# A column sum over 32,768 rows: float32 loads folded in place instead of loads that cast to float16

## The chip, the cores and the metric

The kernel runs on one core of a Trainium2 chip. A core has five engines with their own instruction queues: TensorE (PE in the profile; PEld is its weight load), VectorE (DVE), ScalarE (ACT), GpSimd (POOL) and SyncE (SP). Any of SP, ACT and POOL can issue a DMA; 16 DMA engines carry them out. The metric is the device time of one execution in microseconds (us), the median of several runs.

## The reference

```python
batch, seq, dim = 32, 1024, 2048
grad_output = randn(batch, seq, dim)            # float32
out = np.sum(grad_output, axis=(0, 1))          # float32, 2048 numbers
```

The input is seen as a matrix of 32,768 rows and 2048 columns, 268.4 MB; the output is the sum of each column, 8 KB.

## The kernel before

**The layout.** SBUF has 128 partitions, so 128 rows are one row block; there are 256 blocks of 1.05 MB of float32. A load of `m` blocks puts `m` consecutive rows into each partition, one contiguous run of `m` times 8 KB in memory. To add over the 128 partitions, TensorE multiplies the data with a column of ones (L161): the result is one row of 512 column sums in PSUM. Four PSUM banks (`accs`, L110) hold the four quarters of the 2048 columns, and every matmul accumulates into its bank, from the first with `start` to the last with `stop`.

**The plan (L60 to L85).** A list of loads is made first and then carried out in order (L132 to L168):

- two single blocks in float32, issued by SP (`PRE_TILES`, L62), with tiles of their own;
- thirty loads of eight blocks, and a remainder of two blocks, issued by POOL into float16 tiles `t` (L67): the DMA casts on the way, so that half of what is read is written;
- a taper of four and two blocks (`BULK_TAPER`, L72);
- five single blocks (`TAIL_TILES`, L76);
- the last block in four column pieces, the last quarter first (L80).

Three buffers (`T_BUFS`) take the loads of several blocks. The framework derives all waits between engines from what each instruction reads and writes.

**The work on a tile.** For a tile of several blocks VectorE adds its second half to its first (L152, float16 in and out, into one of three tiles `c`), which halves what TensorE must read; then one matmul (L161) for every 512 columns of `c`: sixteen for eight blocks. A single block goes to TensorE without an add. A buffer is free for the next load as soon as the add at L152 has read it, and POOL's issue (L146) waits for that.

**The end.** Four copies bring the banks from PSUM to the SBUF row `res`, on ScalarE (L175) and VectorE (L177) in turn, the last quarter first; SP stores the 8 KB (L178).

Of the kernel before, what the change touches and what calls it, by code (L numbers as in the profile page):

```python
# [1 line left out]

# [4 lines left out]

P = 128
MM_N = 512  # L10

PRE_TILES = 2
PRE_M = 1
PRE_ENGS = ("sync", "sync")
BULK_M = 8
BULK_TAPER = (4, 2)
USE_DVE = True
TAIL_TILES = 5
COL_SPLIT_LAST = True
T_BUFS = 3  # L20
C_BUFS = 3
TAIL_BUFS = 8
BULK_ENGS = ("gpsimd",)
OUT_COPY_ENGS = ("scalar", "vector")


@with_exitstack
def kernel(
    ctx: ExitStack,
    tc: tile.TileContext,  # L30
    grad_output: bass.AP,
    out: bass.AP,
):
    nc = tc.nc
    fp32 = mybir.dt.float32
    fp16 = mybir.dt.float16

    D = out.shape[-1]
    flat = grad_output.rearrange("b s d -> (b s) d")
    R = flat.shape[0]  # L40
    assert R % P == 0 and D % MM_N == 0
    nbanks = D // MM_N
    n_row_blocks = R // P

    pre_tiles = min(PRE_TILES, n_row_blocks // PRE_M // 4)
    col_split = COL_SPLIT_LAST and nbanks > 1
    taper = [m for m in BULK_TAPER if m < BULK_M]
    n_small = TAIL_TILES + (1 if col_split else 0)
    while pre_tiles * PRE_M + sum(taper) + n_small > n_row_blocks:
        if TAIL_TILES and n_small > 1:  # L50
            n_small -= 1
        elif taper:
            taper = taper[1:]
        else:
            col_split = False
            n_small = min(n_small, 1)
            break
    n_tail = n_small - (1 if col_split else 0)

    plan: list = []  # L60
    row = 0
    for i in range(pre_tiles):  # L62
        plan.append((row, PRE_M, fp32, PRE_ENGS[i % len(PRE_ENGS)], 0, D))
        row += P * PRE_M
    tail_start = R - P * (n_small + sum(taper))
    bi = 0
    while row < tail_start:  # L67
        take = min(P * BULK_M, tail_start - row)
        plan.append((row, take // P, fp16, BULK_ENGS[bi % len(BULK_ENGS)], 0, D))
        bi += 1  # L70
        row += take
    for m in taper:  # L72
        plan.append((row, m, fp16, BULK_ENGS[bi % len(BULK_ENGS)], 0, D))
        bi += 1
        row += P * m
    for _ in range(n_tail):  # L76
        plan.append((row, 1, fp16, BULK_ENGS[bi % len(BULK_ENGS)], 0, D))
        bi += 1
        row += P
    if col_split:  # L80
        for b in range(nbanks - 1, -1, -1):
            plan.append((row, 1, fp16, BULK_ENGS[bi % len(BULK_ENGS)], b * MM_N, MM_N))
            bi += 1
        row += P
    assert row == R  # L85

    io_pool = ctx.enter_context(tc.tile_pool(name="io", bufs=T_BUFS))
    pre_pool = None
    if pre_tiles:
        pre_pool = ctx.enter_context(tc.tile_pool(name="pre", bufs=pre_tiles))  # L90
    c_pool = None
    if USE_DVE:
        c_pool = ctx.enter_context(tc.tile_pool(name="csum", bufs=C_BUFS))
    n_small_tiles = n_tail + (nbanks if col_split else 0)
    tail_pool = None
    if n_small_tiles:
        tail_pool = ctx.enter_context(
            tc.tile_pool(name="tail", bufs=min(n_small_tiles, TAIL_BUFS))
        )
    const_pool = ctx.enter_context(tc.tile_pool(name="const", bufs=1))  # L100
    psum_pool = ctx.enter_context(tc.tile_pool(name="psum", bufs=1, space=bass.MemoryType.PSUM))

    ones16 = const_pool.tile([P, 1], fp16)
    nc.vector.memset(ones16[:], 1.0)  # L104
    ones32 = None
    if pre_tiles:
        ones32 = const_pool.tile([P, 1], fp32)
        nc.vector.memset(ones32[:], 1.0)  # L108

    accs = [  # L110
        psum_pool.tile([1, MM_N], fp32, tag=f"psum{b}", name=f"psum{b}")
        for b in range(nbanks)
    ]
    res = const_pool.tile([1, D], fp32)

    def uses_dve(entry) -> bool:
        _, m, dt_, _, _, col_n = entry
        return USE_DVE and dt_ is fp16 and m > 1 and col_n == D

    def n_chunks(entry) -> int:  # L120
        _, m, dt_, _, _, col_n = entry
        n = (m * col_n) // MM_N
        return n // 2 if uses_dve(entry) else n

    total_mm = [0] * nbanks
    for e in plan:
        for j in range(n_chunks(e)):
            total_mm[((e[4] + j * MM_N) % D) // MM_N] += 1
    started = [False] * nbanks
    n_mm = [0] * nbanks  # L130

    for i, entry in enumerate(plan):  # L132
        row0, m, dt_, eng_name, col_lo, col_n = entry
        rows = flat[row0 : row0 + m * P]
        if col_n == D:
            src = rows.rearrange("(p m) d -> p (m d)", p=P)
        else:
            src = rows[:, col_lo : col_lo + col_n]

        if dt_ is fp16:  # L140
            big = m > 1 and col_n == D
            pool, tag = (io_pool, "T") if big else (tail_pool, "Ttail")
            T = pool.tile([P, m * col_n], fp16, tag=tag, name=f"t{i}")
        else:
            T = pre_pool.tile([P, m * col_n], fp32, tag="Tpre", name=f"t{i}")
        getattr(nc, eng_name).dma_start(out=T[:], in_=src)  # L146

        red = T
        if uses_dve(entry):
            half = (m * col_n) // 2  # L150
            C = c_pool.tile([P, half], fp16, tag="C", name=f"c{i}")
            nc.vector.tensor_tensor(  # L152
                out=C[:], in0=T[:, :half], in1=T[:, half:], op=mybir.AluOpType.add
            )
            red = C

        w = ones16 if dt_ is fp16 else ones32
        for j in range(n_chunks(entry)):
            b = ((col_lo + j * MM_N) % D) // MM_N
            n_mm[b] += 1  # L160
            nc.tensor.matmul(  # L161
                accs[b][:, :],
                lhsT=w[:],
                rhs=red[:, j * MM_N : (j + 1) * MM_N],
                start=(not started[b]),
                stop=(n_mm[b] == total_mm[b]),
            )
            started[b] = True  # L168

    bank_order = list(range(nbanks - 1, -1, -1)) if col_split else list(range(nbanks))  # L170
    for k, b in enumerate(bank_order):
        eng = OUT_COPY_ENGS[k % len(OUT_COPY_ENGS)]
        dst = res[:, b * MM_N : (b + 1) * MM_N]
        if eng == "scalar":
            nc.scalar.copy(out=dst, in_=accs[b][:, :])  # L175
        else:
            nc.vector.tensor_copy(out=dst, in_=accs[b][:, :])  # L177
    nc.sync.dma_start(out=out[None, :], in_=res[:])  # L178


# [1 line left out]
_INS = ['grad_output']  # L182
_OUTS = [((2048,), 'float32')]


# [23 lines left out]
```

## Time and profile before

The times of three runs were 629.38, 629.17 and 629.12 us; the median is 629.17 us. The profiled execution has a span of 627.2 us from its first to its last instruction. The median lies 2.0 us above that; the list of times does not say which of its values belongs to the profiled execution.

| | before |
|---|---|
| median of the runs | 629.17 us |
| span of the profiled execution | 627.2 us |
| written into SBUF by DMA | 135.36 MB, mean 216 GB/s |
| mean granted clock of TensorE | 0.650 of full speed |
| 8-block loads, issue to landing | 53.1 us (median of 30) |
| add at L152, 128x8192 | 4425 ns, 30 times |
| add at L152, 128x4096 | 2293 ns, once |
| matmul instructions on float32, 128x512 | 16, mean 859 ns |
| matmul instructions on float16 sums, 128x512 | 496, mean 533 ns |

How to read the profile: a *busy* share is the time in which an engine executed, over the span. In the *chain that ended last*, the profile goes back from the last instruction to whatever released it, again and again; what stands there set the time. "DVE c L152" is VectorE's instruction of line 152 that writes the tile `c`; "another core or an unknown queue" is a wait whose releaser the profile can't name. In a timeline line the numbers are the start in us from the span's beginning, the busy time, the engine, the line, the operation, and in brackets how long the engine sat idle before and what ended that. In a *stage table* each line is a stretch of time with the busy time and the number of instructions of each engine, the granted clock of TensorE, the busy share of the DMA engines and the GB/s that they wrote. A lower clock makes a matmul longer: the clock switches between half and full speed.

### The profile page before, as it was taken

The numbers are of one execution on the slowest core, as the hardware profiler recorded it, in microseconds if no ns is written. First come the engines' busy times: TensorE is split into PE (matmuls) and PEld (weight loads), VectorE is DVE, ScalarE is ACT, GpSimd is POOL, SyncE is SP. The second block draws the span as 40 slices with busy tenths as digits, with TensorE's granted clock in tenths as the row PEclk, the third lists the DMA queues.
The fourth block names the chain that finished last, engine by engine and source line by source line (L and its number), as shares of the span: only waits on it lengthen the run. The fifth ranks groups of instructions, "written<-read, shape, count | busy, mean of one in ns | idle before, by whom it ended". The sixth has DMA issues, their size and how long they took to land.

```text
span 627.2 us, 1267 instructions
## 1 busy us (share of the span) xinstructions
PE 195.1 (31%) x536; PEld 58.1 (9%) x536; DVE 138.9 (22%) x37; ACT 2.4 (0%) x3; POOL 22.6 (4%) x46
## 2 busy tenths in 40 slices
PE   3323320333203333123341134321333312343165
PEld 0001100011000111001110011100111000111011
DVE  0202222022220122211222202222022221122320
ACT  0000000000000000000000000000000000000000
POOL 1000000000000000000000000000000000000110
PEclk9677556775567665667655776656676567665677
DMA  9999999999999999999999999999999999999997
GB/s 242 226 234 201 234 201 234 202 232 203 232 203 232 203 232 203 232 204 230 205 230 205 230 205 230 205 230 206 228 207 228 207 224 211 224 211 221 206 206 139
DMA packets 6344, 135.36 MB, mean 216 GB/s; under 512 B 705, under 2 KB 1217, under 8 KB 1857
## 3 DMA queue, kind: packets, MB, share of 16 engines
q0 software_dynamic: 6048, 133.17, 98.9%
q1 hardware_dynamic: 290, 2.11, 0.9%
q8 instruction: 4, 0.07, 0.0%
q14 instruction: 2, 0.02, 0.0%
HBM read 268.44 MB, written 0.01 MB: 428 GB/s over the span
## 4 chain that ended last, share of the span: by engine, by line
another core or an unknown queue 66%; DVE 21%; DMA 11%; PE 1%; POOL 1%; issue 0%; DVEq 0%; POOLq 0%
DVE c L152 20%; DMA t<-in_grad_output_dram 11%; PE psum L161 1%; POOL t L146 1%; DVEq L152 0%; DVE res L177 0%; POOLq L193 0%
## 5 line engine op out<-in xcount | busy, mean ns | idle before, releaser
L161 PE MATMUL psum<-c,ones 128*1 128x512 f16 x496 | 175.9, 533 | 405.5 <-DVE c L152 405.5
L152 DVE TENSOR_TENSOR c<-t 128x8192 f16<-128x8192 f16 (+2 forms) x33 | 137.5, 4167 | 471.1 <-DMA t<-in_grad_output_dram 471.1
L161 PEld LDWEIGHTS <-ones 128*1 128x1 f16 x520 | 56.5, 109 | 537.5 <-issue 516.4
L146 POOL DMA_DIRECT2D t<-in_grad_output_dram x42 | 22.4, 538 | 590.4 <-DVE c L152 575.3
L161 PE MATMUL psum<-t,ones 128*1 128x512 f16 (+1 forms) x40 | 19.4, 639 | 23.5 <-DMA t<-in_grad_output_dram 23.5
L177 DVE COPY res<-psum 1x512 f32<-1x512 f32 x2 | 1.4, 679 | 13.9 <-PE psum L161 13.9
L161 PEld LDWEIGHTS psum<-t,ones 128*1 128x1 f32 x16 | 1.6, 106 | 27.5 <-DMA t<-in_grad_output_dram 14.1
L175 ACT COPY res<-psum 1x512 f32<-1x512 f32 x2 | 1.1, 575 | 621.1 <-PE psum L161 621.1
L175 ACT ACT_TABLE_LOAD x1 | 1.3, 1283 | 0.7 <-PEq L193 0.7
L104 DVE MEMSET ones<- 128x1 f16 x1 | 0.1, 59 | 0.8 <-PEq L193 0.8
L193 POOL MEMSET const-float32-0.0<- 128x1 f32 x1 | 0.1, 100 | 0.2 <-issue 0.2
L193 POOL MEMSET const-bfloat16-1.0<- 128x1 bf16 x1 | 0.1, 103 | 0.0
L193 POOL MEMSET const-float32-1.0<- 128x1 f32 x1 | 0.1, 100 | 0.0
L193 POOL MEMSET const-uint8-127<- 128x1 uint8 x1 | 0.1, 100 | 0.0
L108 DVE MEMSET ones<- 128x1 f32 x1 | 0.1, 59 | 0.0
## 6 DMA issues: line engine op xcount, KB each, us to landing
t<-in_grad_output_dram POOLq DMA_DIRECT2D x30, 4096.0 KB, 53.1
t<-in_grad_output_dram POOLq DMA_DIRECT2D x5, 512.0 KB, 20.4
t<-in_grad_output_dram SPq DMA_DIRECT2D x2, 1024.0 KB, 14.3
t<-in_grad_output_dram POOLq DMA_DIRECT2D x2, 1024.0 KB, 26.6
t<-in_grad_output_dram POOLq DMA_DIRECT2D x1, 2048.0 KB, 29.0
t<-in_grad_output_dram POOLq DMA_DIRECT2D x4, 128.0 KB, 16.1
out_dram<-res SPq DMA_DIRECT2D x1, 8.0 KB
```

The source lines that it names most:

```text
L104: nc.vector.memset(ones16[:], 1.0)
L108: nc.vector.memset(ones32[:], 1.0)
L146: getattr(nc, eng_name).dma_start(out=T[:], in_=src)
L152: nc.vector.tensor_tensor(out=C[:], in0=T[:, :half], in1=T[:, half:], op=mybir.AluOpType.add)
L161: nc.tensor.matmul(accs[b][:, :], lhsT=w[:], rhs=red[:, j * MM_N : (j + 1) * MM_N], start=(not started[b]), stop=(n_mm[b] == total_mm[b]),)
L175: nc.scalar.copy(out=dst, in_=accs[b][:, :])
L177: nc.vector.tensor_copy(out=dst, in_=accs[b][:, :])
L193: nc = _bacc.Bacc("TRN2", target_bir_lowering=False, num_devices=1)
```

## The change

The kernel is written anew around a ring, with its own semaphores in place of the derived waits.

- **Loads.** All 256 blocks are loaded as float32, without a cast, and all loads are issued by SP. The ring has three slots of eight blocks, 64 KB of each partition. The units are 29 of eight blocks, then 6, 4, 4, 2, 2, 2, 2 (`UNITS`); unit `i` goes into slot `i % 3`, and from the fourth on SP waits until the unit three before it is used up (`s_free`). The last two blocks come in three pieces: the left three quarters of the columns of both, then the last quarter of each. These use the free part of slot 2 and have no wait of their own.
- **Folds.** VectorE adds in place, float32: blocks 4 to 7 onto 0 to 3 (128x8192), then blocks 2 and 3 onto 0 and 1 (128x4096), with a wait for the first add between them. A 6-block unit adds blocks 4 and 5 onto 0 and 1 and then folds as a unit of four; a 4-block unit has only the second add; a 2-block unit has none. Two blocks are left of every unit.
- **Matmuls.** Eight float32 matmuls for a unit, two for each quarter of the columns. The quarters use four column groups of the TensorE array (`tile_position`) and write to partitions 0, 32, 64 and 96 of PSUM: quarters 0 to 2 into `acc`, quarter 3 into `accr`. Both are cleared by VectorE at the start and every matmul adds. The second four end with the increment that frees the slot; then come six float16 matmuls on zeros into a bank that nothing reads (`FILL`).
- **Loops.** VectorE's first 27 units are a loop of nine turns over the three slots; the rest is written out. TensorE's 36 units are a loop of twelve turns, six fill matmuls in every unit.
- **The end.** The left columns of the last two blocks are summed first; VectorE copies `acc` and SP stores those three quarters while the last quarter is still coming in. After the last quarter's matmuls ScalarE copies `accr` and issues the store of 2 KB itself.

All of it stands in a critical section, in which the framework adds no waits of its own; POOL leads it. The core of the new code:

```diff
+M = 8
+SLOTS = 3
+LOOPS = 9
+UNITS = (M,) * 29 + (6, 4, 4, 2, 2, 2, 2)
+FILL = 6
...
+    def take(engine, sem, n):
+        engine.wait_ge(sem, n)
+        engine.sem_inc(sem, -n)
...
+    def fold(at, n, by):
+        part = ring[:, at : at + n * D]
+        return v.tensor_tensor(
+            out=part, in0=part, in1=ring[:, at + by * D : at + (by + n) * D], op=add
+        )
...
+    def unit(s, m):
...
+        at = s * W
+        take(v, landed[s], 16)
+        if m == 2:
+            v.sem_inc(red[s], 1)
+            return
+        if m > 4:
+            fold(at, *((4, 4) if m == 8 else (2, 4))).then_inc(s_vec, 1)
+            take(v, s_vec, 1)
+        fold(at, 2, 2).then_inc(red[s], 1)
...
+    def sums(at, c0=0, w=D):
+        for g in range(4):
+            lo, hi = max(c0, g * Q), min(c0 + w, (g + 1) * Q)
+            if lo < hi:
+                mm = t.matmul(
+                    (acc if g < 3 else accr)[32 * g : 32 * g + 1, lo - g * Q : hi - g * Q],
+                    lhsT=ones[:],
+                    rhs=ring[:, at + lo - c0 : at + hi - c0],
+                    start=False,
+                    stop=False,
+                    tile_position=(0, 32 * g),
+                    skip_group_check=True,
+                )
+        return mm
...
+    with tc.tile_critical(sync_engine=lead):
...
+        for i, m in enumerate(UNITS):
+            at = i % SLOTS * W
+            src = flat[row * P : (row + m) * P].rearrange("(p m) d -> p (m d)", p=P)
+            if i >= SLOTS:
+                q.wait_ge(s_free, i - SLOTS + 1)
+            q.dma_start(out=ring[:, at : at + m * D], in_=src).then_inc(landed[i % SLOTS], 16)
+            row += m
+        src = flat[row * P :].rearrange("(p m) d -> p m d", p=P)
+        at = (SLOTS - 1) * W + 2 * D
+        left = ring[:, at : at + 6 * Q].rearrange("p (m c) -> p m c", m=2)
+        q.dma_start(out=left, in_=src[:, :, : 3 * Q]).then_inc(last[0], 16)
+        for m in range(2):
+            q.dma_start(
+                out=ring[:, at + (6 + m) * Q : at + (7 + m) * Q], in_=src[:, m, 3 * Q :]
+            ).then_inc(last[1 + m], 16)
...
+        with v.Fori(0, LOOPS) as _:
+            for s in range(SLOTS):
+                unit(s, M)
+        for i in range(LOOPS * SLOTS, len(UNITS)):
+            unit(i % SLOTS, UNITS[i])
...
+        t.wait_ge(s_one, 4)
+        with t.Fori(0, len(UNITS) // SLOTS) as _:
+            for s in range(SLOTS):
+                take(t, red[s], 1)
+                sums(s * W)
+                sums(s * W + D).then_inc(s_free, 1)
+                for _ in range(FILL):
+                    t.matmul(
+                        junk[0:1, :],
+                        lhsT=fill[:, :1],
+                        rhs=fill[:],
+                        start=True,
+                        stop=True,
+                        tile_position=(0, 0),
+                    )
+        t.wait_ge(last[0], 16)
+        sums(at, 0, 3 * Q)
+        sums(at + 3 * Q, 0, 3 * Q).then_inc(s_end[0], 1)
+        for m in range(2):
+            t.wait_ge(last[1 + m], 16)
+            mm = sums(at + (6 + m) * Q, 3 * Q, Q)
+        mm.then_inc(s_end[1], 1)
...
+        v.wait_ge(s_end[0], 1)
+        v.tensor_copy(out=res[0:96, :], in_=acc[0:96, :]).then_inc(s_res[0], 1)
+        a.wait_ge(s_end[1], 1)
+        a.copy(out=res[96:97, :], in_=accr[96:97, :]).then_inc(s_res[1], 1)
+        q.wait_ge(s_res[0], 1)
+        q.dma_start(
+            out=out[: 3 * Q].rearrange("(g c) -> g c", g=3), in_=res[0:65:32, :]
+        ).then_inc(s_out[0], 16)
+        a.wait_ge(s_res[1], 1)
+        a.dma_start(out=out[None, 3 * Q :], in_=res[96:97, :]).then_inc(s_out[1], 16)
```

## The prediction

> **What bounds the kernel now.** I read the busy shares first, then the chain that ended last, then the same chain in order of time, then the end of the timeline. The page's shares and queues:
>
> ```profile
> PE 195.1 (31%) x536; PEld 58.1 (9%) x536; DVE 138.9 (22%) x37; ACT 2.4 (0%) x3; POOL 22.6 (4%) x46
> DMA  9999999999999999999999999999999999999997
> ...
> q0 software_dynamic: 6048, 133.17, 98.9%
> q1 hardware_dynamic: 290, 2.11, 0.9%
> ...
> HBM read 268.44 MB, written 0.01 MB: 428 GB/s over the span
> ```
>
> No compute engine is busy a third of the span; the 16 DMA engines are never idle. 133 MB is written but 268 MB is read, because the bulk loads turn float32 into float16 on the way. The chain in order of time shows the beat (start, length, what):
>
> ```profile
> 46.74 4.43 DVE c L152
> 51.16 14.87 another core or an unknown queue
> 66.06 4.43 DVE c L152
> ...
> 104.81 4.42 DVE c L152
> 109.23 15.75 another core or an unknown queue
> 125.10 4.42 DVE c L152
> 129.53 14.72 another core or an unknown queue
> 144.37 4.42 DVE c L152
> ...
> 588.89 4.43 DVE c L152
> ```
>
> The "unknown queue" is the load stream: L152 starts once per 8-row tile when it lands. From 46.74 to 588.89 are 28 beats. One is long (104.81 to 125.10, 20.29 us); the other 27 average (542.15 - 20.29) / 27 = 19.33 us, or 2.416 us for one row block (128 rows, 1.05 MB read, 434 GB/s). L152 is busy 4.43 us of a beat, so its cost does not set the time. The end, from the timeline (start, busy, engine):
>
> ```profile
> 613.11 1.02 PE L161 MATMUL psum<-t,ones 128*1 128x512 f16 x4 [0.68 <-DMA t<-in_grad_output_dram]
> 615.58 1.02 PE L161 MATMUL psum<-t,ones 128*1 128x512 f16 x4 [1.45 <-DMA t<-in_grad_output_dram]
> 618.02 1.53 PE L161 MATMUL psum<-t,ones 128*1 128x512 f16 x4 [1.42 <-DMA t<-in_grad_output_dram]
> 620.52 3.57 PE L161 MATMUL psum<-t,ones 128*1 128x512 f16 x8 [0.96 <-DMA t<-in_grad_output_dram]
> 624.13 0.68 DVE L177 COPY res<-psum 1x512 f32<-1x512 f32 x1 [0.17 <-PE psum L161]
> 624.90 0.32 SPq L178 DMA_DIRECT2D out_dram<-res  x1
> ```
>
> Single blocks become usable every 2.47 us, so the last block, which follows 620.52 in four pieces, is complete near 623.0. Its matmuls end at 624.09, the last copy at 624.81, the store is issued at 624.90, and the span ends 2.3 us later at 627.2. The median run is 629.17, so 2.0 us lie around the span (629.12 to 629.38 in the list: 1.9 to 2.2); the list does not say which of them the profile belongs to. I carry 2.0 over.
>
> **The change part by part.**
>
> **The load stream.** The same 268.44 MB are read, now written as float32: 8.39 MB into SBUF for a tile instead of 4.19. No row shows 8-row loads of this kind. The nearest are the two one-block float32 loads on SP: the first was issued at 0.74 and its matmul started at 5.74; and while they run, the stage table has
>
> ```profile
> 2.00:6.00 4.00, 0.26 (x1) 0.12 (x2) 0.00 (x0) 0.02 (x1) 0.96 (x2) 1.00 1.38 438
> ```
>
> 438 GB/s landed in SBUF (last column), against the 217 of the bulk, so a doubled write is not slower by itself. Shorter slices of that stage gave 426, 426 and 415. From one side, then, the price is 268.44 MB / 426 GB/s = 630.1 us, 11.6 more than 256 x 2.416 = 618.5; from the other, the shortest beat in the fence (125.10 to 144.37, 19.27 us) gives 616.6. I take 618.5, because the read of 434 GB/s is what the bulk is paced by and it is unchanged.
>
> **The queue.** 42 issues leave POOL (22.4 us busy, off the chain). SP gets 36 loads and three pieces, and the last quarter's store goes to ScalarE's queue, behind its own copy; in front of each from the fourth on stands the wait for a free slot. Behind that wait are only later loads and the first output store, so a late slot delays the stream and nothing else. A slot comes free after two folds and eight matmuls. The trace has no float32 add. The float16 one of 128x8192 took 4425 ns and of 128x4096 2293 ns; at the same time per element both folds would be 6.7 us; at the rate of the float32 copy at L177 (679 ns for 512, 1.33 ns each) 16.3 us; at the same bytes per ns, 2 x (4.43 + 2.29) = 13.4 us. I take 13.4, the row nearest in kind; even 16.3 is under the 19.33 beat.
>
> The Trainium skill ("VectorE: DVE Perf Modes", Mode 2x_2P) says that a float32 tensor_tensor cannot leave the one-element-per-cycle mode; by its 0.96 GHz an estimate of both folds is 12.8 us, which would change nothing in the sum.
>
> **The matmuls.** A float32 one of 512 columns is two matmul instructions in the trace (16 for the two early tiles' eight). Their weight loads start 0.86 us apart up to 27.57 and 0.43 after 28.16, the two clocks. Eight per tile are then 16 x 0.86 = 13.8 us, or 6.9, if the four column groups take turns, and 4 x 0.43 = 1.7 us if four run at once at full clock (3.4 at half). No column group appears in this trace, so both stand. The six fill matmuls are 0.23 us each (16 in 3.61 us) or 0.43: 1.4 to 2.6 us. In the steady state it does not matter: 13.4 + 13.8 = 27.2 us from landing to free, plus about 2.6 from issue to data (5.74 - 0.74 less one block of 2.45), against 38.7 us that the two other slots keep the queue filled. That is the cover, 8.9 us deep.
>
> **The loops.** VectorE's nine and TensorE's twelve turns have branches that the trace does not price. The long beat is the one disturbance it shows, 0.96 us over the others. At that price TensorE's twelve would be 11.5 us if each stopped the stream, and zero if it falls in idle time; in the steady state TensorE works at most 16.4 of 19.33 us, so I take zero.
>
> A rule against the loops: the Trainium skill ("Runtime: NRT & Kernel Launch", Instruction fetch mechanics) says that a taken branch leaving the current two-page window stalls for a fetch; no run here shows one yet. By it the sum would grow only where a turn's code is longer than that window.
>
> **The short units at the end.** The last seven units are 6, 4, 4, 2, 2, 2, 2 blocks, then two blocks in three pieces. Count from when unit 28 is usable. Unit 31 is usable at 14 x 2.416 = 33.8, folded 4.4 later at 38.2. Unit 34 reuses its slot and must be issued 2.6 + 4.8 before 48.3, at 40.9: with 1.7 us of matmuls the slot is free at 39.9, with 3.4 at 41.6, 0.7 late. Unit 35 must be issued at 45.7: free at 43.0 (39.9 + 1.4 of fill + 1.7), or at 47.6 at half clock, 1.9 late. Bounds 0 to 1.9, taken 0.3, because the fills keep TensorE at 3.1 of each 4.8 us. In the stage table TensorE was busy 5.01 of 7 us from 604 to 611 and had a clock of 0.96 in the next 7 us; there it was busy 3.47 of 7, and the clock was 0.53 after 618. 64% lies between 72% and 50%, so either clock can be had.
>
> **The two ends.** The loads stand in a critical section led by POOL; SP's waits around barriers are 0.5 to 0.7 us in the list of waits, so its entry costs 0 to 0.7, taken 0.3. Last quarter: one float32 matmul, 0.86 us (1.7 at half clock) and 0.1 to hand over; ScalarE's copy 0.57 (L175); 0.1 to issue; 2.3 to the end as now. The table load (1283 ns, now at 0.74) stays early if it is ahead of ScalarE's wait; behind it, it adds 1.3. I take zero.
>
> **Sum.** 0.74 + 0.3 + 2.6 + 618.5 = 622.1; + 0.3 slots = 622.4; + 0.96 + 0.57 + 0.1 + 2.3 = 626.3. Against 627.2 that is 0.9 less: 0.6 of the last data (622.4 for 623.0) and 0.3 of the end. With 2.0 around it: 628.3 us, 0.1% under the median, inside the 0.2% (1.26 us) that I count as no change. If every bound falls well (entry and slots 0) it is 627.7; if all go badly (entry 0.7, slots 1.9, half clock, table load behind the wait) 632.5. Half of the difference between the beats of 19.33 and 19.27 lets it reach 626.8.
>
> **Rivals.**
> *TensorE becomes the bound at the end.* Place: units 31 to 35. It decides once matmuls and fills of a two-block unit exceed 4.83 us. If each matmul's second instruction must wait for its first in the same group and only neighbours overlap, eight take 9 x 0.43 = 3.9, with fills 5.2. From 38.2: five units 26.0, the left columns 3.0, two quarters 1.7, end at 68.9 against 58.9: 10.0 more, 638.3. With no overlap: 8.3 a unit, 38.2 + 41.5 + 5.2 + 1.7 = 86.6, about 656. For it: in-order issue and no row with overlap. Against it: four separate column positions. Chance 0.20 (mostly the first).
> *The stream runs at the short slices' rate.* Smaller pieces or pauses between loads on SP: up to 11.6 more, 639.9; with a third of that 632.2. For it: 426 and 415. Against it: those slices hold the first latencies. Chance 0.10.
> *Both ends and the stream gain.* The beat of 19.27 throughout gives 1.9 less, 626.4. For it: PE's unrolled stream, whose fetches I suspect in the long beat, is gone, and so are the short column pieces. Against it: 27 beats average 19.33. Chance 0.10.
>
> **How the numbers follow.** The forecast has 0.60; its own range of 626.8 to 632.5 puts 0.26 below 627.9, 0.31 within 0.2%, 0.03 above 630.4. The fast rival adds 0.10 to faster; the slow two add 0.29 to slower and 0.01 to the same. So 0.36 faster, 0.32 the same, 0.32 slower. Range 625.8 to 638.5: down past the fast rival, up to the partial overlap; no overlap and a stream at 426 are left out.
>
> **What would show it.** Beats between first folds of 19.3 us, folds near 8.9 and 4.5 us, SP never later than the queue's end, DMA at 9 in every slice; in the last 60 us, matmuls of one unit over before the next lands. It is wrong if beats are 19.5 or more, if TensorE works on after the last piece has landed for over 2 us, or if DMA shows gaps before the last units.

## The result, and the profile after

The changed kernel takes 631.11 us (median of six runs, 631.03 to 632.55) against 629.16 us for the kernel before in the same comparison (six runs, 628.64 to 629.38): a ratio of 1.0037, 95% interval 1.0025 to 1.0048. It is slower by 0.37% by that ratio (1.95 us, 0.31%, by the medians), where 628.3 us had been forecast. The profiled execution has a span of 629.3 us and took 631.03, so 1.7 us lie around it; the span itself is 2.1 us longer than the 627.2 of before.

The shares and queues on the page of the changed kernel:

```profile
PE 184.1 (29%) x808; PEld 38.9 (6%) x808; DVE 400.1 (64%) x67; ACT 1.9 (0%) x2; POOL 0.2 (0%) x4
...
DMA  9999999999999999999999999999999999999996
...
q1 hardware_dynamic: 5750, 268.44, 98.9%
...
HBM read 268.44 MB, written 0.01 MB: 427 GB/s over the span
```

VectorE went from 22% to 64% busy and POOL to nothing, and neither shows in the time: the DMA engines are at 9 in every slice but the last, as before. The beat, in the timeline of VectorE (a row is one unit's two folds, of 8.69 and 4.42 us; "DVEq L58" is the wait for a landed load in `take`):

```profile
22.96 13.26 DVE L62 TENSOR_TENSOR ring<-ring 128x8192 f32<-128x8192 f32 x2 [20.45 <-DVEq L58]
...
100.38 13.26 DVE L62 TENSOR_TENSOR ring<-ring 128x8192 f32<-128x8192 f32 x2 [6.09 <-DVEq L58]
119.73 13.27 DVE L62 TENSOR_TENSOR ring<-ring 128x8192 f32<-128x8192 f32 x2 [6.09 <-DVEq L58]
...
564.89 13.26 DVE L62 TENSOR_TENSOR ring<-ring 128x8192 f32<-128x8192 f32 x2 [6.10 <-DVEq L58]
```

From 22.96 to 564.89 are 28 beats, (564.89 - 22.96) / 28 = 19.355 us each. None is long: where before had its 20.29 us beat, this one has 119.73 - 100.38 = 19.35. VectorE waits 6.1 us in every beat, so the folds are not on the path. At 564.89 the first 29 units (232 blocks) are usable. Before, L152's thirtieth tile, with the two early blocks the 242nd block, was usable at 588.89, so 232 blocks at 588.89 - 10 x 2.416 = 564.7. So up to here the two kernels are level to 0.2 us, and the loss lies in the last 65 us. Its first half is in the timeline around unit 31:

```profile
595.41 1.46 PE L131 MATMUL junk<-fill 128*1 128x512 f16 x6
...
595.66 14.60 SPq L101 DMA_DIRECT2D ring<-in_grad_output_dram  x3
598.86 4.42 DVE L62 TENSOR_TENSOR ring<-ring 128x4096 f32<-128x4096 f32 x1 [5.31 <-DVEq L58]
...
603.42 1.03 PE L82 MATMUL acc<-ring,ones 128*1 128x512 f32 x3 [6.55 <-PEq L58]
...
604.23 1.07 PE L82 MATMUL acc<-ring,ones 128*1 128x512 f32 x3
...
605.08 1.07 PE L82 MATMUL acc<-ring,ones 128*1 128x512 f32 x3
...
605.94 0.90 PE L82 MATMUL acc<-ring,ones 128*1 128x512 f32 x3
...
607.97 0.60 PE L82 MATMUL acc<-ring,ones 128*1 128x512 f32 x3
...
608.39 0.60 PE L82 MATMUL acc<-ring,ones 128*1 128x512 f32 x3
```

TensorE had nothing to do for 6.55 us before unit 31. Its matmul instructions then start 0.81 to 0.86 us apart, at half clock; those of unit 32, from 607.5 on, 0.42. Three quarters start as one, and the fourth within 0.03 us of them: the four column groups do run at once. Unit 31's last matmul ends at 605.94 + 0.90 = 606.84, SP issues the load of unit 34 into that slot at 606.92 (the second of the three in the row at 595.66), and its first packet starts at 607.88. The stage table says what the DMA engines did meanwhile (last two columns: their busy share and GB/s):

```profile
606.50:607.00 0.50, 0.50 (x6) 0.17 (x2) 0.00 (x0) 0.00 (x0) 0.00 (x0) 0.96 0.77 328
607.00:607.50 0.50, 0.50 (x4) 0.17 (x2) 0.00 (x0) 0.00 (x0) 0.00 (x0) 1.00 0.70 295
607.50:608.00 0.50, 0.50 (x10) 0.22 (x12) 0.00 (x0) 0.00 (x0) 0.00 (x0) 1.00 1.03 229
```

A packet's time and bytes are booked where it starts, so short slices are rough; still, from the 422 GB/s of the stretch from 595 to 607 they fall to 328, 295 and 229. By the packets' own times unit 33 is in at 608.06 and unit 34 at 614.16, 6.10 us later, where two blocks cost 2 x 2.419 = 4.84: 1.26 us lost. The last packet ends at 624.23, against 622.76 before. The second half of the loss is the end, from the timeline (SPq and ACTq: issues of a DMA):

```profile
623.32 1.03 PE L82 MATMUL acc<-ring,ones 128*1 128x512 f32 x6 [0.39 <-DMA ring<-in_grad_output_dram]
...
625.27 0.69 DVE L149 COPY res<-acc 96x512 f32<-96x512 f32 x1 [21.99 <-PE acc L82]
625.89 0.58 ACT L151 COPY res<-accr 1x512 f32<-1x512 f32 x1 [623.73 <-PE accr L82]
625.99 0.84 SPq L153 DMA_DIRECT2D out_dram<-res  x1
626.50 0.50 ACTq L157 DMA_DIRECT2D out_dram<-res  x1
```

The left columns start at 623.32 and their matmuls, with the last quarter's in turn behind them, keep TensorE until 625.87, 1.64 us after the last packet. So VectorE's copy of the left columns (625.27) and SP's store of them (625.99) come after all data is in, and not while the last quarter is still on its way. By the trace's semaphore records SP's store, issued first, is also the one that lands last: at 627.90, ScalarE's at 627.67. From the last packet to the end of the span are 5.07 us; before they were 627.16 - 622.76 = 4.40.

So the 2.1 us between the two profiled executions are 0.2 up to unit 28, 1.27 from there to the last packet (1.26 of it at unit 34) and 0.67 at the end: 2.14.

### The profile page after: what moved, and what is told of

It reads as the page before. It is cut to its first block, busy times and chain, and to the rows that moved or that the text cites. A ratio compares the mean times of both kernels' runs of the same rounds, so it can differ in the third digit from the quotient of the medians.

```text
span 629.3 us, 1940 instructions
## 1 busy us (share of the span) xinstructions
PE 184.1 (29%) x808; PEld 38.9 (6%) x808; DVE 400.1 (64%) x67; ACT 1.9 (0%) x2; POOL 0.2 (0%) x4
## 5 line engine op out<-in xcount | busy, mean ns | idle before, releaser
L62 DVE TENSOR_TENSOR ring<-ring 128x4096 f32<-128x4096 f32 (+1 forms) x62 | 398.1, 6421 | 202.7 <-DVEq L58 198.3
L82 PE MATMUL acc<-ring,ones 128*1 128x512 f32 x444 | 122.8, 970 | 441.8 <-PEq L58 441.4
L82 PE MATMUL accr<-ring,ones 128*1 128x512 f32 x148 | 121.4, 969 | 0.0
L131 PE MATMUL junk<-fill 128*1 128x512 f16 x216 | 69.4, 471 | 0.0
L82 PEld LDWEIGHTS acc<-ring,ones 128*1 128x1 f32 x444 | 14.9, 100 | 508.1 <-issue 506.6
L131 PEld LDWEIGHTS junk<-fill 128*1 128x1 f16 x216 | 23.2, 107 | 77.4 <-issue 67.8
L82 PEld LDWEIGHTS accr<-ring,ones 128*1 128x1 f32 x148 | 12.0, 100 | 0.6 <-DMA ring<-in_grad_output_dram 0.3
## 6 DMA issues: line engine op xcount, KB each, us to landing
ring<-in_grad_output_dram SPq DMA_DIRECT2D x29, 40.9
```

What stands on the lines that cost most here:

```text
L62: return v.tensor_tensor(out=part, in0=part, in1=ring[:, at + by * D : at + (by + n) * D], op=add)
L82: mm = t.matmul((acc if g < 3 else accr)[32 * g : 32 * g + 1, lo - g * Q : hi - g * Q], lhsT=ones[:], rhs=ring[:, at + lo - c0 : at + hi - ...
L131: t.matmul(junk[0:1, :], lhsT=fill[:, :1], rhs=fill[:], start=True, stop=True, tile_position=(0, 0),)
```

## The experiments

Each comparison has its own runs of the kernel before, on the same chip; "over before" is the difference of the medians in that comparison (it is 1.95 us for the change itself). Spans are quoted beside it. The theory to be tested: the loss is the late slot of unit 34, because TensorE reaches unit 31 at half clock after an idle stretch, and the rest is the new end. The rivals: the store on ScalarE's queue, the fill matmuls, the loops or the sections. "Instruction fetch" stands for packets on the queue that the page calls q8 "instruction".

**1. No slot to wait for (e1).** Units 34 and 35 go into the free halves of slots 1 and 2, so SP issues everything early; TensorE waits for their data itself, and its last turn is written out behind the loop.

```diff
-            at = i % SLOTS * W
+            at = i % SLOTS * W + (4 * D if i >= 34 else 0)
...
-                q.wait_ge(s_free, i - SLOTS + 1)
+                q.wait_ge(s_free, i - (2 if i >= 34 else 1) * SLOTS + 1)
...
-        with t.Fori(0, len(UNITS) // SLOTS) as _:
+        with t.Fori(0, 11) as _:
             for s in range(SLOTS):
+                turn(red[s], s * W)
+        turn(red[0], 0)
+        for k in range(2):
+            turn(late[k], (k + 1) * W + 4 * D, n=16)
```

> Units 34 and 35 are loaded into blocks 4 and 5 of their slots, which have been free since units 28 and 29, so SP has no late wait in front of them; TensorE waits for these two loads itself. Late-slot theory: unit 34's load was issued at 606.92, some 1.5 us after it should have been, and everything behind it is 1.5 us late. So SP issues it right behind unit 33, the DMA engines show no gap near 607.5, and the time falls from 631.1 to 629.6 us, ratio 1.0010 to 1.0015 for 1.0037. Rival, the float32 stream as a whole is slower (beats of 19.36 for 19.33) or the end after the last load is longer: the time stays at 630.9 to 631.2.

Measured: 631.16 us (6 runs), ratio 1.0032 [1.0020, 1.0044], 2.07 over before; span 629.4 in the profile. A miss in time, yet the wait did go: the last load was issued at 599.1, unit 34 was in at 613.13 and the left columns at 621.79, where the change had 614.16 and 622.94. Then one engine was late. Two views of this kernel, the page's queue line and the stage table:

```profile
q8 instruction: 1, 0.02, 0.0%
```

```profile
622.50:623.00 0.50, 0.50 (x6) 0.10 (x3) 0.00 (x0) 0.00 (x0) 0.00 (x0) 1.00 0.57 213
623.00:623.50 0.50, 0.50 (x6) 0.10 (x3) 0.00 (x0) 0.00 (x0) 0.00 (x0) 1.00 0.08 16
623.50:624.00 0.50, 0.50 (x6) 0.00 (x0) 0.00 (x0) 0.00 (x0) 0.00 (x0) 1.00 0.06 12
624.00:624.50 0.50, 0.34 (x4) 0.09 (x2) 0.26 (x1) 0.00 (x0) 0.00 (x0) 1.00 0.04 16
```

A share of 0.06 is one engine of 16. It works alone from 623.1 to 624.40, because a 16 KB instruction fetch at 622.10 took 1.10 us of its time; every load is spread over all 16 and counts as landed when the last of them is done. What was gained at the slot was given back there.

**2. A warm TensorE (e2).** 28 more fill matmuls after unit 30 bridge the idle stretch; the last six turns are written out. The additional work is on zeros.

```diff
+        with t.Fori(0, 10) as _:
             for s in range(SLOTS):
+                turn(red[s], s * W)
+        for i in range(30, 36):
+            turn(red[i % SLOTS], i % SLOTS * W, 34 if i == 30 else FILL)
```

> The slot wait stays, but 28 more fill matmuls (34 for 6) follow unit 30, about 6 us at full clock, so that TensorE is not idle for 6.55 us ahead of unit 31. Late-slot theory with the clock as its cause: unit 31's matmuls run at full clock, 1.7 us for 3.4, slot 1 is free near 605.2 instead of 606.9, and the time falls by 1.2 to 1.5 us to 629.6 to 629.9. Rival, the slot wait is due to the fold or to the queue and not to the clock: the matmuls get shorter but the time stays within 0.3 us of 631.1. If the added fills run at half clock they last 12 us and hold unit 31 up: then about 634.

Measured: 632.02 us (5 runs), 1.0048 [1.0034, 1.0061], 2.93 over before. A miss in time, but half of the theory shows in it: the granted clock is 1.00 from 603 to 607, and SP issues unit 34 at 606.72, 2.11 us after unit 31's fold ends at 604.61; in the change it was 606.92 - 603.28 = 3.64. The fold itself, however, came 1.3 us later (it starts at 600.19, not 598.86), with an instruction fetch at 597.9 ahead of it, and a second fetch at 624.05 stood in the end. The written-out turns brought the fetches, so the time says nothing of the clock alone.

**3. The second store on SP (e3), and no fills (e4).** e3 moves the wait and the store of L157 from ScalarE's queue to SP's; e4 sets `FILL` to 0, which leaves out only the work on zeros.

```diff
-        a.wait_ge(s_res[1], 1)
-        a.dma_start(out=out[None, 3 * Q :], in_=res[96:97, :]).then_inc(s_out[1], 16)
+        q.wait_ge(s_res[1], 1)
+        q.dma_start(out=out[None, 3 * Q :], in_=res[96:97, :]).then_inc(s_out[1], 16)
```

> SP issues the store of the last quarter in place of ScalarE, behind its own store of the first three. Store theory: from the store's issue to the end it took 2.8 us by ScalarE's queue against 2.3 by SP's before, so 0.3 to 0.5 us are saved, less up to 0.4 because SP is busy with its first store until 626.83: 630.6 to 631.0 us. Rival, the longer end belongs to the critical section and not to the queue: 631.1 to 631.5, since the store is issued later.

Measured: 631.65 us (5 runs), 1.0043 [1.0030, 1.0057], 2.56 over before. SP issues the second store at 627.16, behind the 0.84 us of its first; ScalarE had done so at 626.50. ScalarE's queue is not what the end lost by; in the change its store has landed 0.24 us ahead of SP's own.

```diff
-FILL = 6
+FILL = 0
```

> No fill matmuls; what is left out is only the work on zeros that nothing reads. In the steady state nothing changes in either theory. Late-slot theory: unit 31's matmuls are at half clock with or without fills (TensorE is idle 6.55 us ahead of them), so unit 34 is as late as now; units 32 to 35 and the last quarter lose the full clock, units 34 and 35 start without fills in front of them, and the time lies between 630.8 and 632.5. If the fills themselves hold the slots up, the time falls by 1 us or more.

Measured: 631.43 us (5 runs), 1.0038 [1.0024, 1.0051], 2.34 over before. SP issues unit 34 at 606.97, the same as with fills: unit 31 meets a half clock either way (0.50 from 603 to 607).

**4. The late slots again with shorter turns (e1b: `FILL` 2; e1c: `FILL` 0).** Edits as in e1.

> As e1_late_slots, but with two fill matmuls a unit in place of six, so that TensorE's program is 48 matmuls shorter. Theory of the lagging engine: in e1 the wait was gone and the data came 1 us earlier, but TensorE's longer program fetched 16 KB of instructions at 622.1, which held one of the 16 DMA engines up by 1.1 us; here no fetch falls at the end, all pieces have landed near 623.0, and the time is 629.7 to 630.2 us. Rival, the late slot never mattered because something else at the end takes as long: 631.0 to 631.5 again.

Measured: 630.77 us (8 runs), 1.0029 [1.0018, 1.0039], 1.79 over before; the fetch comes again, at 621.84. Fifteen engines are done by 622.75, one at 623.90.

> As e1b_late_short with no fills at all, TensorE's program 48 more matmul entries shorter. If the fetch of 16 KB near 622 comes from the length of TensorE's program, it is gone, all engines end together near 623 and the time is 629.6 to 630.3. If it comes from the code after the loop whatever its length, one engine ends 1.1 us late again and the time is 630.5 to 631.2.

Measured: 630.92 us (7 runs), 1.0037 [1.0025, 1.0048], 2.17 over before; fetch at 621.94. With 6, 2 and 0 fills it falls within 0.3 us of the same moment, so it is not the length of a turn that brings it but the code behind the loop (the change, e12 below and e4, with 6, 2 and 0 fills and no such code, have no fetch); why there and then is not settled.

**5. Other units at the end (e8), one section (e9).** e8 orders the tail as 4, 4, 4, 2, 4, 2, 2 with `FILL` 2. e9 moves SP's wait for the stores into the first critical section (the second `with` is taken out).

```diff
-UNITS = (M,) * 29 + (6, 4, 4, 2, 2, 2, 2)
-FILL = 6
+UNITS = (M,) * 29 + (4, 4, 4, 2, 4, 2, 2)
+FILL = 2
```

> The same short loops and the same slots, but the last units are 4, 4, 4, 2, 4, 2, 2 blocks with two fills, so that a unit of four always has at least six blocks of transfers behind it before its slot is needed. Late-slot theory: unit 34 waits for unit 31, whose turnaround of about 10 us from landing is now covered by 14.5 us of transfers; no gap in the DMA engines; the last data comes near 623, but TensorE gets the fold of unit 33 late and ends 0.5 to 1.5 us after its usual distance: 629.9 to 630.9. Rival, the time is set elsewhere: 631.1 to 632.

Measured: 631.82 us (5 runs), 1.0042 [1.0028, 1.0056], 2.84 over before. A miss: the gap only moved, to 583 (66 GB/s from 583.0 to 583.5). Unit 31 waits there for unit 28's slot, whose matmuls at 579.66 are again 0.85 us apart. The last packet ends at 624.41.

```diff
-    with tc.tile_critical(sync_engine=mybir.EngineType.SP):
         for s in s_out:
             q.wait_ge(s, 16)
```

> The waits for the two stores stand inside the one critical section and not in a second one led by SP. After the last store landed near 627.9 the changed kernel has 1.3 us of barriers to its end, the kernel before 0.8. Section theory: 0.4 to 0.6 us saved, 630.5 to 630.7. Rival, POOL's part in the exit is what is long, whichever section it is: 631.0 to 631.3.

Measured: 631.42 us (5 runs), 1.0045 [1.0031, 1.0058], 2.44 over before; 1.2 us still follow the landing of the last store. No gain.

**6. Both loops written out (e5).** VectorE's and TensorE's; the work is the same.

```diff
-        with v.Fori(0, LOOPS) as _:
-            for s in range(SLOTS):
-                unit(s, M)
-        for i in range(LOOPS * SLOTS, len(UNITS)):
+        for i in range(len(UNITS)):
             unit(i % SLOTS, UNITS[i])
```

> Both loops written out. Fetch theory: TensorE's program of about 1100 instructions is fetched in 16 KB pieces as in the kernel before (four pieces there), each of which sets one DMA engine back by 1.1 us for good; one beat in the middle is about 1 us longer. The slot wait at the end stops the other 15 engines for about as long, so the lag is hidden behind it: 631.1 to 631.7. If lags add up on one engine, 633 or more; if the loops' branches had cost anything, the time falls below 630.8.

Measured: 633.05 us (5 runs), 1.0065 [1.0052, 1.0079], 4.07 over before, above the 631.1 to 631.7 of the fetch theory; its queue line on the page:

```profile
q8 instruction: 6, 0.10, 0.1%
```

Six fetches (157.3, 292.8, 391.8, 505.6, 598.6 and 607.8 us), where the change has none, and the last packet ends at 625.45 instead of 624.23. The loops are worth about 2.1 us by the medians (4.07 less 1.95), 1.2 by the spans of the profiled runs (630.5 for 629.3). Part of it is that the lagging engines and the late slot add up: SP issues unit 34 at 608.04, and the stream is thinned from 607 to 609 (33 GB/s in the last half microsecond of that), longer than in the change.

**7. Only unit 34 early, the loop untouched (e11; e12 with `FILL` 2).** Unit 34 goes into the free half of its slot. VectorE copies it to where TensorE's loop expects it, so that no code stands behind the loop.

```diff
-            at = i % SLOTS * W
+            at = i % SLOTS * W + (4 * D if i == 34 else 0)
...
+            if i == 34:
+                v.wait_ge(late, 16)
+                v.wait_ge(s_free, 32)
+                v.tensor_copy(
+                    out=ring[:, W : W + 2 * D], in_=ring[:, W + 4 * D : W + 6 * D]
+                ).then_inc(red[1], 1)
+                continue
             unit(i % SLOTS, UNITS[i])
```

> Only unit 34 is loaded into the free half of its slot; VectorE, idle by then, copies it to the slot's first two blocks once unit 31 is used up, so TensorE's looped program is unchanged and no instructions are fetched. Late-slot theory: no gap in the DMA engines near 607.5, no engine left behind, last data at 622.8 to 623.0 for 624.2, and the time falls by 1.0 to 1.4 us to 629.7 to 630.2 (span 628.0 to 628.3 for 629.3). Rival, the loads are not what the end waits for: 631 again.

Measured: 630.15 us (11 runs), 1.0022 [1.0013, 1.0031], 1.40 over before; span 628.5 in the profile. Its copy in the timeline, and its stage table:

```profile
613.71 2.29 DVE L126 COPY ring<-ring 128x4096 f32<-128x4096 f32 x1 [10.15 <-DMA ring<-in_grad_output_dram]
```

```profile
606.50:607.00 0.50, 0.50 (x5) 0.01 (x1) 0.00 (x0) 0.00 (x0) 0.00 (x0) 0.60 1.00 426
607.00:607.50 0.50, 0.50 (x7) 0.24 (x3) 0.00 (x0) 0.00 (x0) 0.00 (x0) 1.00 1.00 426
607.50:608.00 0.50, 0.50 (x7) 0.19 (x9) 0.00 (x0) 0.00 (x0) 0.00 (x0) 1.00 0.78 328
...
623.00:623.50 0.50, 0.50 (x7) 0.18 (x5) 0.00 (x0) 0.00 (x0) 0.00 (x0) 1.00 0.06 21
```

426 GB/s where the change had 328 and 295; unit 34 is in 4.88 us after unit 33 (613.20 - 608.32), against 6.10. There is no fetch, and the last packet ends at 623.20, 1.03 us sooner. The median is 0.96 lower, 0.55 if each is taken over its own comparison's kernel before, and there the two intervals overlap. The versions that keep both the slot wait and TensorE's loop (the change, e3, e4, e8, e9) lie 1.95 to 2.84 over before; this one and the next, 1.40 and 1.42. Of the 1.4 us of span still lost against before, 0.44 lie ahead of the last packet and 0.93 behind it (5.33 for 4.40). The matmuls of unit 31 are still at half clock (0.51 from 603 to 607): it is the dependence on them that went.

> The same with two fill matmuls a unit for six. Both theories of the end expect the same as for e11_late_copy within 0.4 us; if the fills delay units 34, 35 and the left columns, it is up to 0.5 us faster, and if they are needed for the clock at the end, up to 0.8 us slower.

Measured: 630.17 us (11 runs), 1.0022 [1.0013, 1.0031]: the same, and the fills do not matter here either.

**8. Without column groups (e6).** All quarters at column position 0, in four banks.

```diff
-                    (acc if g < 3 else accr)[32 * g : 32 * g + 1, lo - g * Q : hi - g * Q],
+                    accs[g][0:1, lo - g * Q : hi - g * Q],
...
-                    tile_position=(0, 32 * g),
+                    tile_position=(0, 0),
```

> All four quarters of the columns use column position 0, each with a PSUM bank of its own (three copies at the end in place of one, 1.4 us more). Overlap theory: the trace shows four column groups starting within 0.03 us of each other; without it a unit's matmuls take 16 x 0.43 = 6.9 us and with fills 8.3, more than the 4.8 us in which two blocks arrive, TensorE works on long after the last data, and the time is 650 to 660 us, while the beats of the 8-block units stay 19.36. Rival, the groups don't matter: 632 to 634.

Measured once: 658.76 us, span 656.6. In the list of waits VectorE's final copy waits for TensorE 46.3 us, against 22.0 in the change:

```profile
DVE res L149 <- PE acc L81: 46.3, 1, 46.3
```

This is the prediction's rival without overlap, which it priced at 656. The four column positions, then, are worth some 26 us at the end: 27.6 in all, less what two more copies cost (1.4 by the expectation).

**9. The left columns as two loads (e13).** e11 with the piece of the last two blocks split and one section.

```diff
-        left = ring[:, at : at + 6 * Q].rearrange("p (m c) -> p m c", m=2)
-        q.dma_start(out=left, in_=src[:, :, : 3 * Q]).then_inc(last[0], 16)
+        for m in range(2):
+            q.dma_start(
+                out=ring[:, at + 3 * m * Q : at + 3 * (m + 1) * Q], in_=src[:, m, : 3 * Q]
+            ).then_inc(last[3 * m], 16)
```

> e11_late_copy, with the left columns of the last two blocks as two loads, so that the first block's are summed 1.8 us earlier, and with the store waits in the one section. After the last data e11 needs 5.2 us to the end, the kernel before 4.4. Theory that the end after the last data is what is left: 0.3 to 0.8 us off, 629.4 to 629.9. Rival, these steps are hidden behind the last quarter and the barriers: 630.0 to 630.4.

Measured: 630.9 us (6 runs, 629.71 to 632.25), 1.0032 [1.0019, 1.0044], 1.83 over before. Inconclusive: the spread covers the effect. In the profiled run the end did get shorter: SP's store is issued at 624.78 and lands at 626.69, now ahead of ScalarE's (627.31), and 4.71 us follow the last packet, for 5.33 in e11. But that packet ends at 623.88, 0.68 later than in e11, for a reason that is not settled, and the two changes of this run are not told apart.

**10. The kernel before with a shorter TensorE program (b1).** If fetches cost the kernel before some 1.1 us, fewer matmuls should win it back. VectorE, which had 15 us to spare in a beat, folds each tile to one block in float16 and adds four such blocks; TensorE sees one block for four tiles. All rows are still summed, with more of the adding in float16.

```diff
+                nc.vector.tensor_tensor(
+                    out=C[:, :half], in0=C[:, :half], in1=C[:, half : 2 * half],
+                    op=mybir.AluOpType.add,
+                )
...
+                    nc.vector.tensor_tensor(
+                        out=run[:], in0=run[:], in1=C[:, :D], op=mybir.AluOpType.add
+                    )
```

> The kernel before, with VectorE folding each tile of several blocks to one block and adding four tiles together before TensorE sums them, so that TensorE has 146 program entries for 1050. Fetch theory: the kernel before loses 1.1 us because fetches of TensorE's instructions set single DMA engines back for good (from 113.9 us on); without them there is no long beat, the DMA engines end together about 1 us earlier, and the time is 627.6 to 628.3 for 629.0, ratio 0.998 to 0.999. Rival, the long beat has another cause or the end waits for something else: 628.8 to 629.4.

Measured: 628.03 us (11 runs), ratio 0.9985 [0.9976, 0.9994], 1.04 under before: the fastest version of this study, ahead of both kernels. The timeline of VectorE, at the place of the long beat:

```profile
104.68 4.43 DVE L158 TENSOR_TENSOR c<-t 128x8192 f16<-128x8192 f16 x1 [10.05 <-DMA t<-in_grad_output_dram]
...
124.02 4.42 DVE L158 TENSOR_TENSOR c<-t 128x8192 f16<-128x8192 f16 x1 [10.52 <-DMA t<-in_grad_output_dram]
```

124.02 - 104.68 = 19.34: the long beat is gone, and the page has no q8 line. A shorter one is left, in the chain in order of time:

```profile
239.98 4.43 DVE c L158
...
259.31 4.44 DVE c L158
268.12 10.95 another core or an unknown queue
279.09 4.44 DVE c L158
```

From 259.31 to 279.09 are 19.78 us, 0.45 over its neighbours, and at 273.39 the trace has an 8 KB packet on a second queue called "instruction" (q14). After it one engine ends each tile 0.45 us behind the rest: half the bytes, and about half the lag of a 16 KB fetch. TensorE's instructions fell from 536 to 84 matmuls, the VectorE share rose to 44%. This run changes the adds and the matmuls together with the fetches; that it is the fetches rests on the place of the gain, on this smaller copy of it, and on e5 and e1, where added fetches cost. In the profiled executions the span is 0.5 us shorter, what a lag of 0.94 (see below) less these 0.45 would give; the rest of the 1.04 is within the interval.

## Why the prediction was wrong

Its sum was 626.3 us of span and came to 629.3. Of the 3.0 us, 2.7 lie in three terms, and 0.2 to 0.3 come back around the span (1.7 to 1.8 for 2.0). The step whose reasoning failed is the short units; in the ends the path was wrong as well, and the stream's term was only mis-sized.

**The load stream** (618.5, with 0.74 + 0.3 + 2.6 in front): right in kind, and a little short. The first issue is at 0.88 (entry 0.14, taken 0.3), data is usable 2.7 us plus a unit later. But the beat was 19.355 and not 19.33: 256 x 2.4193 = 619.4, 0.9 more than the term. Against before this is nearly neutral, since the prediction's 19.33 leaves out the long beat, which the kernel before did pay. Without 16 KB fetches the float16 loads of b1 keep 19.33 (from 104.68 to 259.31); whether the doubled bytes or the other queue make up the 0.03 us is not settled. The stream rival (a third or all of the way to 426 GB/s) is false: 8 x 1.0486 MB / 19.355 us = 433 GB/s.

**The short units** (bounds 0 to 1.9, taken 0.3, measured 1.26): the step that failed. The prediction gave both branches, 0.7 late for unit 34 at half clock and none at full, and chose near the second "because the fills keep TensorE at 3.1 of each 4.8 us". That is the share in two-block units. Unit 31 is a four-block unit behind another, 9.7 us and a fold later, and TensorE was idle for 6.55 us before it. Its own reckoning at half clock was close: slot free at 41.6 us after unit 28, measured 606.84 - 564.89 = 41.95, and the issue at 42.03. Against the 40.9 that it gave as the latest that is 1.1 late, which is nearly the 1.26 us lost. Unit 35, which it feared most, was issued at 609.93 - 564.89 = 45.04, ahead of its 45.7. e11, which removes the dependence and adds a copy of 2.29 us on VectorE, takes 1.03 us off the last packet. That half clock comes from the idle stretch is shown by e2 (clock 1.00, SP 1.5 us sooner after the fold).

**The two ends** (0.96 + 0.57 + 0.1 + 2.3 = 3.9, an expected gain of 0.3): measured from usable data (the last landing, 0.3 after the last packet in both kernels) 629.26 - 624.54 = 4.7. The path was wrong here. The prediction followed the last quarter alone, to ScalarE's store. But the left columns land only 1.26 us before the last quarter (623.28 and 624.54), and their matmuls stand ahead in TensorE's order, so 1.35 us went by for the 0.96 until ScalarE could copy. And what the end waits for is the other branch: VectorE's copy at 625.27, SP's store, which is 0.84 us in the issuing (0.32 before) and lands at 627.90, 0.24 behind ScalarE's. Then 1.35 us follow that landing, 0.88 before. Nearly all of this difference lies on SP, between the end of its wait for the store and its part in the last barrier: 0.55 us for 0.10, and still 0.40 in e9 with one section. From the issue of the store that lands last to the end these are 3.3 us, for "2.3 as now".

**The folds** (13.4 us taken; 8.69 + 4.42 = 13.1), **the queue** (SP never late before unit 34) and **the matmuls** in the steady state were right: 8 of them, 16 instructions in four steps, take 1.7 us at full and 3.4 at half clock, the price for four at once. POOL's issues before were not quite off the chain, as the prediction read it: the page gives L146 1% of it. The rival in which TensorE becomes the bound fails by that; e6 shows what it would have cost.

**The loops** were costed at zero, which is right for the branches (e5, without them, is no faster) and misses what they spare. The window from 113 to 115 us of the kernel before, inside its long beat, has this queue line:

```profile
q8 instruction: 1, 0.02, 3.0%
```

Such a fetch falls at 113.9, 268.5, 425.4 and 577.6 us, some eight tiles apart, and a tile has 16 matmuls with their 16 weight loads: eight tiles make 256 instructions. From the packets' times, the engines end a tile within 0.2 us of each other ahead of 113.9 and 1.14 apart after it, a lag of 0.94, and they stay so: nothing in the trace takes work off the engine that carried the fetch. After the second and third fetch two and three engines are behind, by the same amount, so these cost no further beat. The Trainium skill ("Runtime: NRT & Kernel Launch", Instruction fetch mechanics) says that programs are fetched in blocks of 16 KiB, 256 instructions, at a cost "mostly hidden"; the size and the interval agree with this trace. On TensorE, idle for two thirds of the time, the cost does not show, but on the DMA side it does: b1 gains 1.04 us without the 16 KB fetches, e5 loses 2.1 with six. The prediction's fast rival named the fetches and gave the gain at most 0.10 of the chance, yet the change does hold that gain, and it is what offsets the slower beat. The same page's rule against branches, weighed in the prediction, did not bite here: the loops ran without one fetch.

## What to carry to other kernels

In a ring of few slots the last, short units need their own reckoning: work out for each when the slot it reuses is free, with TensorE at half clock if it has waited for several microseconds before (after 6.55 us here; after 1.73 us, ahead of unit 35, it was still at full); an issue 1.1 us late cost 1.26 us that did not come back. Where DMA sets the time, look for instruction fetches among the queues: each one here put a single DMA engine back for the rest of the stream (in e5 until the late slot, where the others had to wait too), so a shorter program (a loop with little code behind it, or fewer matmuls) can be worth about a microsecond, where VectorE's share going from 22% to 64% did not show. And a last piece that is split so that most of it is summed early gains only if that sum, its copy and its store are over before the rest lands; otherwise its store can be the last to land, as here.

## What the runs showed of the hardware

- One 16 KB instruction fetch takes 0.9 to 1.1 us of one of the 16 DMA engines, and the lag stays: ends of the engines 0.2 us apart before, 1.14 after (kernel before), one engine working alone for 1.3 us (e1) and 1.2 us (e1b). An 8 KB one put an engine 0.45 us back (b1).
- Float32 matmuls in four column groups run at once: the four quarters' instructions start together, a step every 0.42 us at full and 0.85 us at half clock, two steps for four matmuls of 128x512. In one column position the kernel took 27.6 us more.
- The float32 add in place of 128x8192 took 8692 ns, 1.96 times the 4425 of the float16 one of the same shape.
- A queue that had run dry took 0.96 us from SP's issue to the first packet, and unit 34's two blocks took 6.28 us from first packet to last (607.88 to 614.16), where the ones before and after took 5.3 to 5.5.
